# One adaLN / HGRN2 / stick-breaking / SwiGLU layer in float32: GpSimd's elementwise work on VectorE, conditioning rows in one operation each, 1 MB loads in a ring of 8 KB tiles

## The chip, the cores and the metric

The kernel runs on one core of one Trainium2 chip. The metric is the device time of one execution in microseconds (us). A core has TensorE (PE, matmuls; PEld is its weight load), VectorE (DVE), ScalarE (ACT), GpSimd (POOL) and SyncE (SP), which issues the DMAs of this kernel. The "granted clock" is the share of TensorE's full clock that the profile shows for a stretch.

## The reference

One layer, 512 tokens, width 2048, hidden width 5632, all float32. Cut to what matters:

```python
cond = silu(c)
mod = cond @ w_ada + b_ada                     # 6 rows of 2048: sh1, sc1, g1, sh2, sc2, g2
h = rms_norm(x, norm1_g) * (1 + sc1) + sh1
proj = h @ w_in                                # columns: hgrn2 q, f, i, g; attention q, k, v
o_hg = hgrn2_mixer(...)                        # gated linear recurrence, 8 heads of 128
o_sb = stick_breaking_mixer(...)               # causal stick-breaking attention, 8 heads of 128
x = x + g1 * (concat(o_hg, o_sb) @ w_out)
h = rms_norm(x, norm2_g) * (1 + sc2) + sh2
gate, up = split(h @ w_ffn_in)
x = x + g2 * ((silu(gate) * up) @ w_ffn_out)
```

The product cond @ w_ada is a matrix times one vector; it reads 100 MB for 12288 sums.

## The kernel before, in words

**Matmuls in pieces.** TensorE multiplies a float32 matrix in a reduced form, so each operand is split into a high part (a cast, on ACT) and the remainder (a subtraction, mostly on DVE). A product is three matmuls: high x high, high x low, low x high (`three`, L207). `weights` (L197) loads a piece of 512 KB at most (`raw`, a ring of four tiles of 4 KB per partition, shared by nearly all loads of the kernel), casts it (L203) and subtracts (L204). A new load waits until the tile four loads before it has been read for the last time; SP issues in order, so a load that waits holds up those behind it.

**Conditioning rows.** `gemv` (L179) makes one row of 128 sums: two halves of 512 KB on SP (L176), for each a multiply with `cond` that also sums (L183), into half_a and half_b. `ada` adds the halves and b_ada (L189) and for the two scale rows makes the gain (L192). There are 96 such rows and 14 more of the same form (`fix`).

**Stages in order of time.** A, `st`, L265 to L297: 16 steps over the input width for the `i` columns of all HGRN2 heads, with one SC1 row, one piece of x and 512 KB of weights per step and 24 matmuls 512 wide. x isn't normalised yet; the sums of squares are gathered beside it, ss1, by GpSimd (L288). B: `sb_project(0)` and `sb_project(1)`, q, k and v of attention heads 0 and 1, eight chunks of 24 matmuls 384 wide each (tiles wsb_0 to wsb_7, accumulated in sbp). Beside them run, as side tasks, the 16 SH1 rows and `first_norm`, in which GpSimd multiplies x by the row norm rb (L471). When these are done, hhi and hlo, TensorE's operand, are rewritten with the normalised and shifted input (L486 to L488). C: `sb_project` of heads 2 to 7, and all attention (`sb_attend`: transposes tA and tB, products sbo; L373 scales q and k, L345 the output). In C the parts that A and B computed from the raw input are repaired: `spread` writes a row to memory and reads it back on all partitions (drow), `fix` makes 14 rows with it, and `settle` adds the result to heads 0 and 1 and to the `i` columns. Then HG (HGRN2, eight heads), `wo` (output projection; `split_o`, L773, splits the mixer's output, odd pieces on GpSimd), a first part of the FFN, the FFN loop over f = 2 to 43 (seven products of 24 matmuls 256 wide per f, from sums and differences of the weight quarters), and `fo`, the last product.

**Order.** The order in which TensorE takes projection, attention and repair work is made when the program is written out: a planner's clock counts matmul time, and a side task (a generator) goes on when the clock has reached the time that it asked for. Y holds these delays; "settle" is the one between the last fix of a group and its settle. A head whose rows reuse a buffer waits for the head that holds it (`reuse`, L307: head 3 waits for head 0).

Of the kernel before, what the change touches and what calls it, by code (L numbers as in the profile page):

```python
# [128 lines left out]
def trunk(ctx, tc, a):  # L129
# [41 lines left out]

    ahead = {}

    def gemv_load(src, i, name):
        w = raw_tile([P, 1024], f"{name}_{i}")
        nc.sync.dma_start(w, src[:, i * 1024:i * 1024 + 1024])  # L176
        return w

    def gemv(src, row, col_a, col_b, name):  # L179
        for i, col in enumerate((col_a, col_b)):  # L180
            w = ahead.pop((name, i)) if (name, i) in ahead else gemv_load(src, i, name)
            sl = slice(i * 1024, i * 1024 + 1024)
            V.scalar_tensor_tensor(w, w, 1.0, row[:, sl], op0=ALU.mult, op1=ALU.mult, accum_out=col)  # L183

    def ada(comp, k):
        j = comp * KT + k
        c = slice(j, j + 1)
        gemv(a["w_ada"][j], cond, half_a[:, c], half_b[:, c], f"ada{j}")
        V.scalar_tensor_tensor(mod[:, c], half_a[:, c], half_b[:, c], small_col(C_BADA, j), op0=ALU.add, op1=ALU.add)  # L189
        if comp in (SC1, SC2):  # L190
            g, base = (gain1, C_N1) if comp == SC1 else (gain2, C_N2)
            V.scalar_tensor_tensor(g[:, k:k + 1], mod[:, c], 1.0, small_col(base, k), op0=ALU.add, op1=ALU.mult)  # L192

    def mcol(comp, k):
        return mod[:, comp * KT + k:comp * KT + k + 1]

    def weights(src, shape, name):  # L197
        r = raw_tile(shape, name + "r")
        nc.sync.dma_start(r, src)
        hi = wp.tile(shape, F32R, tag="hi", name=name + "h")  # L200
        lo = wp.tile(shape, F32R, tag="lo", name=name + "l")
        with tc.high_priority(offset=AHEAD):
            S.copy(hi, r)  # L203
            V.tensor_sub(lo, r, hi.bitcast(F32))  # L204
# [60 lines left out]
    for k in range(KT):  # L265
        xk = xo[:, k]
        if k == 0:
            ada(SC1, k)
            whi = wp.tile([P, 1024], F32R, tag="hi", name="wi0h")
            wlo = wp.tile([P, 1024], F32R, tag="lo", name="wi0l")  # L270
            for sl in (slice(0, T), slice(T, 2 * T)):
                S.copy(whi[:, sl], w0[:, sl])
                V.tensor_sub(wlo[:, sl], w0[:, sl], whi[:, sl].bitcast(F32))
        else:
            nc.sync.dma_start(xk, a["x"][:, k])
            ada(SC1, k)
            if k == 2:
                nc.sync.dma_start(cst, a["cst"])
            whi, wlo = weights(a["w_hi"][k], [P, 1024], f"wi{k}")
        gk = gain1[:, k:k + 1]  # L280
        S.activation(hhi[:, k], xk, AF.Identity, scale=gk)
        V.scalar_tensor_tensor(hlo[:, k], xk, gk, hhi[:, k].bitcast(F32), op0=ALU.mult, op1=ALU.subtract)
        if k == 0:
            S.activation(ss1, xk, AF.Square)
        else:
            sq = sb.tile([P, T], F32, tag="qT" if k % 2 else "kT", name=f"sq{k}", bufs=1)
            S.activation(sq, xk, AF.Square)
            G.tensor_add(ss1, ss1, sq)  # L288
# [49 lines left out]
    def row_norm_scale(o_ps, name, pool, tp=None):  # L338
# [4 lines left out]
        y = rstd_small(pool, ss, 4, name)  # L343
        for t in range(4):
            V.tensor_scalar(orow[:, t], o_ps[:, t * P:t * P + P], y[:, t:t + 1], None, op0=ALU.mult)  # L345
        yield Y["norm"]
# [13 lines left out]
    def sb_prepare(h):  # L360
# [9 lines left out]
        y = rstd_small(sb, ss, 8, f"sb{h}")  # L370
        for t in range(4):
            for j in range(2):
                V.tensor_scalar(rows[:, t, j * P:j * P + P], rows[:, t, j * P:j * P + P],  # L373
                                y[:, 2 * t + j:2 * t + j + 1], None, op0=ALU.mult)

# [91 lines left out]
    def first_norm():  # L467
        ps = att("ssum")
        rstd_wide(sb, ss1, ps, "n1", ("qT", "L"), 1, rb)
        for k in range(KT):  # L470
            G.tensor_mul(xo[:, k], xo[:, k], rb)  # L471
# [301 lines left out]
    def split_o(k):  # L773
        S.copy(ohi[:, k], xo[:, k])
        (G if k % 2 else V).tensor_sub(olo[:, k], xo[:, k], ohi[:, k].bitcast(F32))
# [103 lines left out]

    def operand(raw, name):  # L880
        hi = wp.tile([P, HALF, P], F32R, tag="hi", name=name + "h")
        lo = wp.tile([P, HALF, P], F32R, tag="lo", name=name + "l")
        with tc.high_priority(offset=AHEAD):
            S.copy(hi, raw)  # L884
            V.tensor_sub(lo, raw, hi.bitcast(F32))
        return hi, lo

    def load_block(pool, tag, bufs, f, g, kh):
        r = pool.tile([P, HALF, P], F32, tag=tag, name=f"ff{f}_{g}{kh}", bufs=bufs)
        nc.sync.dma_start(r, a["w_fi"][f, g][:, kh * HALF:kh * HALF + HALF])  # L890
        return r

    def product(out, w, p, first=False):
# [241 lines left out]
```

## Time and profile before

| What | us |
|---|---|
| median of three runs (2403.39 to 2404.9) | 2404.03 |
| the profiled execution | 2405.08 |
| its span in the profile (granted clock 0.993) | 2403.3 |
| A begins | 11.2 |
| B begins | 109.2 |
| C begins | 200.7 |
| HG begins | 484 |
| wo begins | 818 |
| FFN loop begins | 1067.3 |
| fo begins | 1920 |

The table's boundaries are the first matmuls of each stage by the timeline, and the windows of the prediction are cut at them. Between the span and the execution's time lie 1.8 us. A row of the timeline reads: start, duration, engine, line, operation, out<-in, shapes, count, and in brackets how long the engine had been idle and what ended that. Successive rows of DVE can overlap by some tens of ns, so the cost of one in a busy row is taken from start to start.

### The profile page before, as it was taken

Reading aid. Unit: us, or ns where it says so; the run is one execution under the profiler, and the core shown is the slowest. Engines: PE = TensorE matmul, PEld = TensorE weight load, DVE = VectorE, ACT = ScalarE, POOL = GpSimd, SP = SyncE. Lnnn points to the kernel's source line nnn. Section 1 sums busy time; section 2 is a strip of 40 time slices with the busy share of each in tenths; the row PEclk is TensorE's granted clock in tenths of the full one; section 3 lists DMA queues with packets and bytes.
Section 4 is the critical chain, followed back from the end, with each engine's and each line's share of the span. In section 5 each row is a group of like instructions: output and inputs, shape, how many; then the busy total and the mean of one; then the engine's idle time right before and its main releaser. Section 6 shows DMA issues by size and latency. Waiting matters only on the chain.

```text
span 2403.3 us, 36514 instructions
## 1 busy us (share of the span) xinstructions
PE 2321.8 (97%) x14371; PEld 2106.9 (88%) x14371; DVE 1701.3 (71%) x2585; ACT 1033.9 (43%) x1833; POOL 82.6 (3%) x64
## 2 busy tenths in 40 slices
PE   7989898999999999989999999999999999999999
PEld 6778788978888778889999999999999988888887
DVE  8997888789888875598888877777777633333332
ACT  4343664466565522374444444444444421122221
POOL 2250000000000200000000000000000000000000
PEclk9999999999999999999999999999999999999999
DMA  8878546743332286535555533333333484363342
GB/s 316 278 248 262 191 156 224 238 165 115 106 106 97 79 266 219 188 121 178 185 184 185 182 135 131 129 130 130 131 132 132 170 327 155 101 198 95 106 127 88
DMA packets 122488, 403.10 MB, mean 168 GB/s; under 512 B 13614, under 2 KB 14284, under 8 KB 122188
## 3 DMA queue, kind: packets, MB, share of 16 engines
q1 hardware_dynamic: 122316, 400.77, 49.8%
q8 instruction: 112, 1.84, 0.3%
q14 instruction: 60, 0.49, 0.1%
HBM read 369.24 MB, written 31.47 MB: 167 GB/s over the span
## 4 chain that ended last, share of the span: by engine, by line
PE 75%; DVE 10%; DMA 9%; issue 3%; ACT 2%; POOL 0%; POOLq 0%; SPq 0%; ACTq 0%; DVEq 0%
PE ffA L92 20%; PE fo L92 20%; PE ffC L92 10%; PE wo L92 6%; PE ffB L92 5%; DMA ada<-in_w_ada 4%; PE hgg L92 3%; DVE ada L183 3%; PE hgf L92 3%; PE hgq L92 3%; PE ff L92 1%; DMA fix<-in_w_fix 1%; DVE I L413 1%; PE l L92 1%; PE hgo L92 1%
## 5 line engine op out<-in xcount | busy, mean ns | idle before, releaser
L183 DVE SCALAR_TENSOR_TENSOR ada<-ada,cond 128x1024 f32<-128x1024 f32 x192 | 260.5, 1366 | 94.9 <-DMA ada<-in_w_ada 94.6
L92 PE MATMUL fo<-act,wfo_0h 128*128 128x512 f32 x1024 | 315.4, 389 | 0.0
L92 PEld LDWEIGHTS fo<-act,wfo_0h 128*128 128x128 f32 x1024 | 192.2, 188 | 39.9
L92 PE MATMUL fo<-act,wfo_0l 128*128 128x512 f32 x512 | 199.2, 389 | 0.0
L204 DVE TENSOR_TENSOR wfo_8l<-wfo_8r,wfo_8h 128x512 fp32r<-128x512 f32 x48 | 33.2, 692 | 177.6 <-ACT wfo_8h L203 177.6
L1071 DVE SCALAR_TENSOR_TENSOR x<-fo,mod,x 128x512 f32<-128x512 f32 x64 | 48.1, 751 | 131.2 <-PE fo L92 127.2
L203 ACT CAST wfo_0h<-wfo_0r 128x1024 fp32r<-128x1024 f32 x64 | 67.7, 1058 | 164.9 <-PE fo L92 142.1
L92 PE MATMUL ffA<-opA,ff_1h 128*128 128x256 f32 x672 | 124.6, 286 | 6.1 <-DVE up L1001 6.1
L92 PE MATMUL ffA<-opB,ff_6h 128*128 128x256 f32 x672 | 124.0, 285 | 2.1 <-ACT ff_6h L884 2.1
L92 PE MATMUL ffC<-opB,ff_7h 128*128 128x256 f32 x672 | 123.1, 283 | 0.4 <-ACT ff_7h L884 0.4
L92 PE MATMUL ffB<-opA,ff_2h 128*128 128x256 f32 x672 | 122.8, 283 | 0.0
L92 PE MATMUL ffA<-opC,ff_5h 128*128 128x256 f32 x672 | 122.8, 283 | 0.0
L92 PE MATMUL ffC<-opC,ff_4h 128*128 128x256 f32 x672 | 122.8, 283 | 0.0
L92 PE MATMUL ffA<-opD,ff_3h 128*128 128x256 f32 x672 | 122.8, 283 | 0.0
L203 ACT CAST wfo_8h<-wfo_8r 128x512 fp32r<-128x512 f32 x48 | 30.0, 624 | 210.3 <-PE fo L92 210.3
L92 PE MATMUL fo<-act,wfo_8h 128*128 128x512 f32 x384 | 118.2, 389 | 0.0
L92 PEld LDWEIGHTS fo<-act,wfo_0l 128*128 128x128 f32 x512 | 96.1, 188 | 19.9
L92 PEld LDWEIGHTS ffA<-opA,ff_1h 128*128 128x128 f32 x672 | 106.4, 195 | 6.3 <-issue 6.3
L92 PEld LDWEIGHTS ffA<-opB,ff_6h 128*128 128x128 f32 x672 | 105.9, 194 | 2.3 <-ACT ff_6h L884 2.3
L92 PEld LDWEIGHTS ffC<-opB,ff_7h 128*128 128x128 f32 x672 | 104.9, 192 | 0.7 <-ACT ff_7h L884 0.7
L92 PEld LDWEIGHTS ffB<-opA,ff_2h 128*128 128x128 f32 x672 | 104.8, 192 | 0.0
L92 PEld LDWEIGHTS ffA<-opC,ff_5h 128*128 128x128 f32 x672 | 104.8, 192 | 0.0
(691 smaller groups left out, 6727.1 us busy)
## 6 DMA issues: line engine op xcount, KB each, us to landing
ada<-in_w_ada SPq DMA_DIRECT2D x192, 512.0 KB, 4.5
ff<-in_w_fi SPq DMA_DIRECT2D x168, 512.0 KB, 3.6
wfo_0r<-in_w_fo SPq DMA_DIRECT2D x64, 512.0 KB, 3.6
actd<-pair SPq DMA_DIRECT2D x44, 512.0 KB, 2.6
act<-actd SPq DMA_DIRECT2D x44, 512.0 KB, 6.2
fix<-in_w_fix SPq DMA_DIRECT2D x28, 512.0 KB, 4.9
wfo_8r<-in_w_fo SPq DMA_DIRECT2D x48, 256.0 KB, 2.7
wo_8r<-in_w_out SPq DMA_DIRECT2D x16, 512.0 KB, 4.4
```

Source lines behind the costliest of these rows:

```text
L92: self.engine.matmul(out, lhsT, rhs, **kw)
L183: V.scalar_tensor_tensor(w, w, 1.0, row[:, sl], op0=ALU.mult, op1=ALU.mult, accum_out=col)
L203: S.copy(hi, r)
L204: V.tensor_sub(lo, r, hi.bitcast(F32))
L413: V.tensor_tensor_scan(Ig[:, ::-1], seg[:, base:base + width][:, ::-1], Lg[:, ::-1], 0.0, op0=ALU.mult, op1=ALU.add)
L1071: V.scalar_tensor_tensor(x2[m], out, mcol(G2, m), x2[m], op0=ALU.mult, op1=ALU.add)
```

## The change

1. GpSimd's sums (ss1), products (xo by rb) and remainders (olo) are made by DVE. GpSimd keeps the memsets.
2. A conditioning row is one load of 1 MB (8 KB per partition) and one multiply-and-sum over 2048 elements straight into its column of mod. b_ada is added for all 16 columns of a component at once when its last row is in (for SC1 still one by one), and the second gain likewise. Only the very first row is still in two halves. The addition of ba and bb falls away with the halves.
3. Weights come in loads of 1 MB or 768 KB (pairs of chunks of w_sb, whole tiles of w_hg, w_out and w_ffn_in, a chunk's whole row of w_ffn_out); each is split in halves as before. The raw ring has four tiles of 8 KB per partition; the FFN's second ring (raw2, five tiles of 4 KB) becomes "sum", two of 4 KB.
4. The scalings per head: one multiply by a broadcast column in place of eight (L373, now L391) or four (L345, now L364).
5. Y["settle"] goes from 8 to 20. The program is also built with dynamic_dma_scratch_size=256.

Lines move: load L176 to L174, gemv L183 to L178, weight load L199 to L205, cast and subtraction L203/L204 (in the FFN L884/L885) to L212/L213, xo by rb L471 to L488, hlo L488 to L505, sums of the FFN quarters L1011 to L1014 to L1022 to L1025.

```diff
-     "settle": 8.0, "shrow": 6.0, "fix": 2.6, "hgtask": 30.0, "task": 5.0}
+     "settle": 20.0, "shrow": 6.0, "fix": 2.6, "hgtask": 30.0, "task": 5.0}
...
-    def gemv(src, row, col_a, col_b, name):
-        for i, col in enumerate((col_a, col_b)):
-            w = ahead.pop((name, i)) if (name, i) in ahead else gemv_load(src, i, name)
-            sl = slice(i * 1024, i * 1024 + 1024)
-            V.scalar_tensor_tensor(w, w, 1.0, row[:, sl], op0=ALU.mult, op1=ALU.mult, accum_out=col)
+    def row_load(src, name):
+        w = raw_tile([P, D], name)
+        nc.sync.dma_start(w, src)
+        return w
+
+    def gemv(w, row, col):
+        V.scalar_tensor_tensor(w, w, 1.0, row, op0=ALU.mult, op1=ALU.mult, accum_out=col)
...
+        gemv(row_load(a["w_ada"][j], f"ada{j}"), cond, mod[:, c])
+        left[comp] -= 1
+        if comp == SC1:
+            V.tensor_add(mod[:, c], mod[:, c], small_col(C_BADA, j))
+            finish_gain(comp, k, k + 1)
+        elif not left[comp]:
+            all_k = slice(comp * KT, comp * KT + KT)
+            V.tensor_add(mod[:, all_k], mod[:, all_k], small[:, C_BADA + comp * KT:C_BADA + comp * KT + KT])
...
-            G.tensor_add(ss1, ss1, sq)
+            V.tensor_add(ss1, ss1, sq)
...
-            whi, wlo = weights(a["w_sb"][h, c], [P, 2, 384], f"wsb{h}_{c}")
+            if c % 2 == 0:
+                raw = load(a["w_sb"][h, c // 2], [P, 2, 2, 384], f"wsb{h}_{c}")
+            whi, wlo = split(raw[:, c % 2], [P, 2, 384], f"wsb{h}_{c}")
...
-        for t in range(4):
-            V.tensor_scalar(orow[:, t], o_ps[:, t * P:t * P + P], y[:, t:t + 1], None, op0=ALU.mult)
+        V.tensor_mul(orow, o_ps.rearrange("p (t d) -> p t d", t=4), view(y, 0, [[1, 4], [0, P]]))
...
+        qk = rows[:, :, 0:2 * P].rearrange("p t (j d) -> p t j d", j=2)
+        V.tensor_mul(qk, qk, view(y, 0, [[2, 4], [1, 2], [0, P]]))
...
-            G.tensor_mul(xo[:, k], xo[:, k], rb)
+            V.tensor_mul(xo[:, k], xo[:, k], rb)
...
-        gemv(a["w_fix"][j], shrow, ba[:, j:j + 1], bb[:, j:j + 1], f"fix{j}")
+        gemv(row_load(a["w_fix"][j], f"fix{j}"), shrow, ba[:, j:j + 1])
...
-        (G if k % 2 else V).tensor_sub(olo[:, k], xo[:, k], ohi[:, k].bitcast(F32))
+        V.tensor_sub(olo[:, k], xo[:, k], ohi[:, k].bitcast(F32))
...
-        A11, A12 = (load_block(wp, "raw", 4, f, 0, kh) for kh in range(2))
-        A21, A22 = (load_block(tp, "raw2", 5, f, 1, kh) for kh in range(2))
-        S1 = tp.tile([P, HALF, P], F32, tag="raw2", name=f"ffS{f}", bufs=5)
+        A11, A12 = halves_of(load(a["w_fi"][f, 0], [P, KT, P], f"wg{f}"))
+        A21, A22 = halves_of(load(a["w_fi"][f, 1], [P, KT, P], f"wu{f}"))
+        S1 = tp.tile([P, HALF, P], F32, tag="sum", name=f"ffS{f}")
```

DVE in stage B at head 1's chunks, before (ada_0 and ada_1 are the two halves of a row, wsb_4l the remainder of the fourth chunk of weights, hlo the rewritten operand):

```order
L204 TENSOR_TENSOR wsb_4l<-wsb_4r,wsb_4h 128x768
L189 SCALAR_TENSOR_TENSOR mod<-half_a,half_b,small 128x1
L183 SCALAR_TENSOR_TENSOR ada_0_1353,half_a<-ada_0_1353,cond 128x1024
L488 TENSOR_TENSOR hlo<-xo,hhi 128x512
L183 SCALAR_TENSOR_TENSOR ada_1_1356,half_b<-ada_1_1356,cond 128x1024
L488 TENSOR_TENSOR hlo<-xo,hhi 128x512
L204 TENSOR_TENSOR wsb_5l<-wsb_5r,wsb_5h 128x768
```

A row's two halves and two rewrites stand between the remainders of two chunks. After, at head 0's chunks, where GpSimd multiplied before (rb is the row norm, rcolT its transpose):

```order
L178 SCALAR_TENSOR_TENSOR ada_945,mod<-ada_945,cond 128x2048
L488 TENSOR_TENSOR xo<-xo,rb_783 128x512 x2
L213 TENSOR_TENSOR wsb_4l<-wsb_4r,wsb_4h 128x768
L213 TENSOR_TENSOR wsb_5l<-wsb_4r,wsb_5h 128x768
L488 TENSOR_TENSOR xo<-xo,rb_783 128x512 x12
L213 TENSOR_TENSOR wsb_6l<-wsb_6r,wsb_6h 128x768
L213 TENSOR_TENSOR wsb_7l<-wsb_6r,wsb_7h 128x768
L488 TENSOR_TENSOR xo<-xo,rb_783 128x512 x2
L494 COPY rcol<-rcolT 128x1 x4
L178 SCALAR_TENSOR_TENSOR ada_978,mod<-ada_978,cond 128x2048
```

The two subtractions of a pair of chunks stand together, the products of xo are among them, and the 16 rewrites of hlo have moved behind the last SH1 row, into stage C.

TensorE at the attention of head 0, before, around its second group of transposes tB (tA is the first group, sbo the products with the values, spread belongs to a settle, sbp is projection work):

```order
L97 MATMUL tB_2080<-cst,I_1844 128x128
L92 MATMUL sbp_1_1869<-wsb_4h,hlo 128x384
L92 MATMUL sbp_2_1870<-wsb_4h,hhi 128x384
L92 MATMUL sbp_2_1870<-wsb_4l,hhi 128x384
L92 MATMUL sbp_2_1870<-wsb_4h,hlo 128x384
L92 MATMUL sbp_3_1871<-wsb_4h,hhi 128x384
L92 MATMUL sbp_3_1871<-wsb_4l,hhi 128x384
L92 MATMUL sbp_3_1871<-wsb_4h,hlo 128x384
L92 MATMUL sbp_0_1868<-wsb_5h,hhi 128x384
L97 MATMUL tB_2080<-cst,L_1843 128x128
```

Projection matmuls of head 3 stand between its steps here. After, from the first transposes tA on:

```order
L92 MATMUL sbp_3_1660<-wsb_7h,hhi 128x384
L92 MATMUL sbp_3_1660<-wsb_7l,hhi 128x384
L97 MATMUL tA_1908<-cst,I_1789 128x128 x2
L97 MATMUL tA_1908<-cst,L_1788 128x128
L97 MATMUL tA_1908<-cst,I_1789 128x128
L92 MATMUL sbp_3_1660<-wsb_7h,hlo 128x384
L92 MATMUL sbo_1932<-scr,L_1788 128x128 x4
L97 MATMUL spread_2016<-cst,ba 3x128
L97 MATMUL tB_1965<-cst,I_1789 128x128
L97 MATMUL tB_1965<-cst,L_1788 128x128
```

Head 0's attention stood inside a projection; now it stands at the end of head 3's, with one projection matmul between its steps.

VectorE in the FFN loop after, from a gemv to the first use of the next f's weights (wu8r, whose tile of the ring the gemv's row had held; ffS is the sum of its halves):

```order
L178 SCALAR_TENSOR_TENSOR ada_10265,mod<-ada_10265,cond 128x2048
L1025 TENSOR_TENSOR wg7r<-wg7r 128x1024
L213 TENSOR_TENSOR ff_6l<-wg7r,ff_6h 128x1024
L1001 TENSOR_TENSOR sg_10022<-sg_10022,up_10023 128x512
L213 TENSOR_TENSOR ff_7l<-wu7r,ff_7h 128x1024
L1004 TENSOR_TENSOR pair_10030<-sg_10022,pair_10030 128x512
L1040 TENSOR_TENSOR sg_10253<-ffB_10043,a_10081 128x256
L1022 TENSOR_TENSOR ffS_10272<-wu8r 128x1024
```

Six operations stand between the two. Before, a row came in two halves at two places of the loop, and the weights of the second block had a ring of their own.

More of the change, by code (lines that the diff above doesn't have):

```diff
@@ L158, in trunk @@
     G.memset(epsb, EPS)
-    half_a = const.tile([P, 96], F32, name="half_a")
-    half_b = const.tile([P, 96], F32, name="half_b")
+    lead = const.tile([P, 2], F32, name="lead")
+    left = [KT] * 6
     mod = const.tile([P, 96], F32, name="mod")
@@ L170, in raw_tile, with finish_gain @@
         return wp.tile(shape, F32, tag="raw", name=name, bufs=4)
[L172 to L176, printed above, removed]
-        return w
-    def gemv(src, row, col_a, col_b, name):
-        for i, col in enumerate((col_a, col_b)):
-            w = ahead.pop((name, i)) if (name, i) in ahead else gemv_load(src, i, name)
-            sl = slice(i * 1024, i * 1024 + 1024)
-            V.scalar_tensor_tensor(w, w, 1.0, row[:, sl], op0=ALU.mult, op1=ALU.mult, accum_out=col)
+    def row_load(src, name):
+        w = raw_tile([P, D], name)
+        nc.sync.dma_start(w, src)
+        return w
+    def gemv(w, row, col):
+        V.scalar_tensor_tensor(w, w, 1.0, row, op0=ALU.mult, op1=ALU.mult, accum_out=col)
+    def finish_gain(comp, k0, k1):
+        g, base = (gain1, C_N1) if comp == SC1 else (gain2, C_N2)
+        V.scalar_tensor_tensor(g[:, k0:k1], mod[:, comp * KT + k0:comp * KT + k1], 1.0, small[:, base + k0:base + k1],
+                               op0=ALU.add, op1=ALU.mult)
     def ada(comp, k):
@@ L187, in ada, with load, split @@
         c = slice(j, j + 1)
[L188 to L192, printed above, removed]
+        gemv(row_load(a["w_ada"][j], f"ada{j}"), cond, mod[:, c])
[6 more added lines that the diff above has]
+            V.tensor_add(mod[:, all_k], mod[:, all_k], small[:, C_BADA + comp * KT:C_BADA + comp * KT + KT])
+            if comp == SC2:
+                finish_gain(comp, 0, KT)
     def mcol(comp, k):
+        assert comp == SC1 or not left[comp]
         return mod[:, comp * KT + k:comp * KT + k + 1]
-    def weights(src, shape, name):
+    def load(src, shape, name):
         r = raw_tile(shape, name + "r")
         nc.sync.dma_start(r, src)
+        return r
+    def split(r, shape, name):
         hi = wp.tile(shape, F32R, tag="hi", name=name + "h")
@@ L205, in weights @@
         return hi, lo
+    def weights(src, shape, name):
+        return split(load(src, shape, name), shape, name)
     def three(out, whi, wlo, xhi, xlo, start, stop):
@@ L252, in trunk @@
     banks += [wide[:, 0:T], wide[:, T:2 * T]]
+    r0 = raw_tile([P, D], "ada_first")
     for i in range(2):
@@ L255, in trunk @@
         nc.sync.dma_start(cond[:, sl], a["c"][:, sl])
-        ahead[f"ada{SC1 * KT}", i] = gemv_load(a["w_ada"][SC1 * KT], i, f"ada{SC1 * KT}")
+        nc.sync.dma_start(r0[:, sl], a["w_ada"][SC1 * KT][:, sl])
         S.activation(cond[:, sl], cond[:, sl], AF.Silu)
@@ L267, in trunk @@
         if k == 0:
-            ada(SC1, k)
+            for i in range(2):
+                sl = slice(i * 1024, i * 1024 + 1024)
+                gemv(r0[:, sl], cond[:, sl], lead[:, i:i + 1])
+            j = SC1 * KT
+            V.scalar_tensor_tensor(mod[:, j:j + 1], lead[:, 0:1], lead[:, 1:2], small_col(C_BADA, j), op0=ALU.add, op1=ALU.add)
+            finish_gain(SC1, 0, 1)
             whi = wp.tile([P, 1024], F32R, tag="hi", name="wi0h")
@@ L370, in sb_prepare @@
         y = rstd_small(sb, ss, 8, f"sb{h}")
[L371 to L374, printed above, removed]
+        qk = rows[:, :, 0:2 * P].rearrange("p t (j d) -> p t j d", j=2)
+        V.tensor_mul(qk, qk, view(y, 0, [[2, 4], [1, 2], [0, P]]))
     def sb_attend(h):
@@ L495, in trunk @@
     ba = const.tile([P, 14], F32, name="ba")
-    bb = const.tile([P, 14], F32, name="bb")
     def spread(dst, cols, n0, n1):
@@ L513, in settle @@
         yield Y["settle"]
-        V.tensor_add(ba[:, n0:n1], ba[:, n0:n1], bb[:, n0:n1])
         spread(brow, ba, n0, n1)
@@ L575, in mtile @@
         n = 0
+        raw = load(src, [P, nk, P], name)
         for c0 in range(0, nk, HALF):
             w = min(HALF, nk - c0)
-            whi, wlo = weights(src[:, c0:c0 + w], [P, w, P], f"{name}_{c0}")
+            whi, wlo = split(raw[:, c0:c0 + w], [P, w, P], f"{name}_{c0}")
             for kk in range(w):
@@ L774, in split_o @@
         S.copy(ohi[:, k], xo[:, k])
-        (G if k % 2 else V).tensor_sub(olo[:, k], xo[:, k], ohi[:, k].bitcast(F32))
+        V.tensor_sub(olo[:, k], xo[:, k], ohi[:, k].bitcast(F32))
     for k in list(range(8, 16)) + list(range(last)):
         split_o(k)
-    wo, wo_n, wo_w = {}, {}, {}
+    wo, wo_n, wo_w, wo_raw = {}, {}, {}, {}
     def wo_part(m, c0, ks):
@@ L785, in wo_part @@
         if (m, c0) not in wo_w:
-            wo_w[m, c0] = weights(a["w_out"][m][:, c0:c0 + 8], [P, 8, P], f"wo{m}_{c0}")
+            if m not in wo_raw:
+                wo_raw[m] = load(a["w_out"][m], [P, KT, P], f"wo{m}")
+            wo_w[m, c0] = split(wo_raw[m][:, c0:c0 + 8], [P, 8, P], f"wo{m}_{c0}")
         whi, wlo = wo_w[m, c0]
@@ L878, in make_second @@
         parts[1, 1, j] = H[3][:, j, 0], H[3][:, j, 1]
[L880 to L891, printed above, removed]
     def product(out, w, p, first=False):
@@ L980, in trunk, with halves_of, operand @@
     actd = [dram.tile([P, 2, T], F32, name=f"actd{f}") for f in range(FM)]
+    def halves_of(r):
+        return r[:, 0:HALF], r[:, HALF:KT]
+    def operand(raw, name):
+        return split(raw, [P, HALF, P], name)
     def tap(src, name):
@@ L1060, in trunk @@
             n = 0
+            raw = load(a["w_fo"][m][:, f0:f0 + size], [P, size, P], f"wfo{c}_{m}")
             for c0 in range(0, size, HALF):
                 w = min(HALF, size - c0)
-                whi, wlo = weights(a["w_fo"][m][:, f0 + c0:f0 + c0 + w], [P, w, P], f"wfo{c}_{m}_{c0}")
+                whi, wlo = split(raw[:, c0:c0 + w], [P, w, P], f"wfo{c}_{m}_{c0}")
                 for kk in range(w):
@@ L1090 @@
     w_in = get["w_in"][0]
-    w_sb = w_in[:, 4096:].reshape(8, 2, P, 3, NH, P).transpose(4, 0, 2, 1, 3, 5).reshape(NH, 8, P, 2, 384)
+    w_sb = w_in[:, 4096:].reshape(4, 2, 2, P, 3, NH, P).transpose(5, 0, 3, 1, 2, 4, 6).reshape(NH, 4, P, 2, 2, 384)
     hgm = mtiles(w_in[:, :4096], KT).reshape(4, NH, P, KT, P)
@@ L1123 @@
     }
-    nc = bacc.Bacc("TRN2", target_bir_lowering=False, num_devices=1)
+    nc = bacc.Bacc("TRN2", target_bir_lowering=False, num_devices=1, dynamic_dma_scratch_size=256)
     args = {n: nc.dram_tensor(f"in_{n}", v.shape, mybir.dt.from_np(v.dtype), kind="ExternalInput").ap()
```

## The prediction

> **What bounds the kernel now.** I read the page's head first, then windows cut at the stages, then the timelines of VectorE and GpSimd inside the slow stages, and last the list of waits.
>
> ```profile
> span 2403.3 us, 36514 instructions
> PE 2321.8 (97%) x14371; PEld 2106.9 (88%) x14371; DVE 1701.3 (71%) x2585; ACT 1033.9 (43%) x1833; POOL 82.6 (3%) x64
> ```
>
> TensorE is 97% busy, so the whole kernel looks bound by it and GpSimd looks irrelevant. Both are averages. The windows by stage (columns: stretch, length, busy us of PE, PEld, DVE, ACT, POOL, granted clock, DMA share, GB/s) say where it isn't so:
>
> ```profile
> 11.20:109.20 98.00, 93.58 (x385) 72.85 (x386) 90.40 (x132) 37.00 (x51) 24.51 (x15) 1.00 0.88 303
> 109.20:200.70 91.50, 76.74 (x401) 69.69 (x400) 83.78 (x124) 39.50 (x57) 34.57 (x16) 0.98 0.79 254
> 1200.00:1240.00 40.00, 40.00 (x336) 40.00 (x335) 34.72 (x43) 19.40 (x28) 0.00 (x0) 1.00 0.53 181
> ```
>
> In the FFN loop (third row) TensorE has no gap, and nothing that the change does to the other engines can pay there. In stage A (the values of eight heads, 16 steps) and stage B (the projections of heads 0 and 1) VectorE is busy 92% of the time, TensorE 95% and 84%. What would TensorE need alone? Its rows start one behind the other, first two of stage A, then two of an undisturbed 384-wide stretch:
>
> ```profile
> 69.38 0.39 PE L92 MATMUL st<-wi9h,hhi 128*128 128x512 f32 x1
> ...
> 71.87 0.39 PE L92 MATMUL st<-wi9h,hlo 128*128 128x512 f32 x1
> ```
> ```profile
> 201.85 0.33 PE L92 MATMUL sbp<-wsb_0h,hhi 128*128 128x384 f32 x1
> ...
> 204.28 0.33 PE L92 MATMUL sbp<-wsb_1h,hlo 128*128 128x384 f32 x1
> ```
>
> Eleven matmuls in 2.49 us are 0.226 us each, and 14 in 2.43 us are 0.174. Stage A has 16 x 24 of the first: 87 us, where it takes 98. Stage B has 2 x 8 x 24 of the second: 67, where it takes 91.5. So 11 and 25 us are above TensorE's floor. What takes them shows in VectorE's and GpSimd's timelines, first for a step of A:
>
> ```profile
> 73.54 2.31 DVE L183 SCALAR_TENSOR_TENSOR ada<-ada,cond 128x1024 f32<-128x1024 f32 x1
> ...
> 75.78 1.21 DVE L183 SCALAR_TENSOR_TENSOR ada<-ada,cond 128x1024 f32<-128x1024 f32 x1
> ```
> ```profile
> 72.98 1.79 POOL L288 TENSOR_TENSOR ss<-ss,sq 128x512 f32<-128x512 f32 x1 [4.31 <-ACT sq L287]
> ```
>
> The same product takes 2.31 us where it meets GpSimd's sum and 1.21 where it doesn't: 1.1 us lost per step. In stage B GpSimd multiplies without a break (16 products, 34.6 us, below), and VectorE reads:
>
> ```profile
> 134.42 1.09 DVE L189 SCALAR_TENSOR_TENSOR mod<-half_a,half_b,small 128x1 f32<-128x1 f32 x1
> 135.44 0.94 DVE L204 TENSOR_TENSOR wsb_4l<-wsb_4r,wsb_4h 128x768 fp32r<-128x768 f32 x1
> 136.31 2.30 DVE L183 SCALAR_TENSOR_TENSOR ada<-ada,cond 128x1024 f32<-128x1024 f32 x1
> ...
> 138.54 2.31 DVE L183 SCALAR_TENSOR_TENSOR ada<-ada,cond 128x1024 f32<-128x1024 f32 x1
> ...
> 141.90 0.94 DVE L204 TENSOR_TENSOR wsb_5l<-wsb_5r,wsb_5h 128x768 fp32r<-128x768 f32 x1
> ...
> 154.83 1.22 DVE L183 SCALAR_TENSOR_TENSOR ada<-ada,cond 128x1024 f32<-128x1024 f32 x1
> ...
> 157.59 0.21 DVE L189 SCALAR_TENSOR_TENSOR mod<-half_a,half_b,small 128x1 f32<-128x1 f32 x1
> ...
> 166.25 0.69 DVE L488 TENSOR_TENSOR hlo<-xo,hhi 128x512 fp32r<-128x512 f32 x1
> 166.85 1.22 DVE L183 SCALAR_TENSOR_TENSOR ada<-ada,cond 128x1024 f32<-128x1024 f32 x1
> ```
>
> A chunk takes 6.46 us (135.44 to 141.90), with VectorE back to back, against 24 x 0.174 = 4.2 of TensorE. Once GpSimd is done the three long operations cost 1.22, 1.22 and 0.21. So stage B has VectorE, slowed by GpSimd, as its bound until 154. After that it waits for loads:
>
> ```profile
> 160.51 1.22 DVE L183 SCALAR_TENSOR_TENSOR ada<-ada,cond 128x1024 f32<-128x1024 f32 x1 [0.97 <-DMA ada<-in_w_ada]
> ```
> ```profile
> 155.00:200.00 45.00, 40.93 (x218) 37.23 (x219) 39.40 (x69) 25.51 (x39) 0.00 (x0) 1.00 0.87 280
> ```
>
> **The change part by part.**
>
> *GpSimd's work on VectorE.* The groups that go:
>
> ```profile
> L471 POOL TENSOR_TENSOR xo<-xo,rb 128x512 f32<-128x512 f32 x16 | 34.6, 2198 | 18.9 <-DVE rb L215 18.9
> L288 POOL TENSOR_TENSOR ss<-ss,sq 128x512 f32<-128x512 f32 x15 | 24.5, 1634 | 72.5 <-ACT sq L287 72.5
> L775 POOL TENSOR_TENSOR olo<-xo,ohi 128x512 fp32r<-128x512 f32 x8 | 13.5, 1705 | 48.8 <-ACT ohi L774 48.7
> ```
>
> A 128x512 operation costs VectorE 0.60 from start to start (166.25 to 166.85). Stage A: 15 x (1.09 lost - 0.60 added), and mod, gain and one accumulator read in fewer pieces, bring 90.4 us of VectorE to about 82. Stage B: 83.8 - 16 x 1.09 + 16 x 0.60 - some 13 rewrites of hlo (0.60 each, moved behind the last SH1 row, which is in stage C) = 68. The Trainium skill, page "SBUF — State Buffer", Terms, has it that VectorE and GpSimd share a pair of ports and that the loser is blocked for the whole instruction. Read as GpSimd's full 2.2 us, 35 us would come back in B; the trace shows 1.09 per meeting, and wsb_4l at 0.94 is not stretched at all, so the sum goes by 1.09. In VectorE's new order twelve of the products stand in a row between wsb_5l and wsb_6l, 7.2 us in which no weight is split; the two chunks ahead keep TensorE busy for 48 x 0.174 = 8.4, so I count nothing, and 1 to 2 us if it reaches them early.
>
> *Loads.* VectorE out of the way, A needs 98.0 x 303 = 29.7 MB and B 91.5 x 254 = 23.2 MB. At full share these rates are 303 / 0.88 = 344 and 254 / 0.79 = 321 GB/s: 86 and 72 us. The other end is what the same queue moves when it never pauses, with 512 KB loads:
>
> ```profile
> 1945.00:1950.00 5.00, 5.00 (x24) 4.14 (x23) 1.89 (x3) 1.06 (x1) 0.00 (x0) 1.00 1.03 406
> ```
>
> At 406 they need 73 and 57. No row shows 8 KB rows, so I take the lower rates, A's and B's own. The Trainium skill, page "DMA: Bandwidth & Descriptors", Bandwidth, tells to batch up to 1 MiB, with 341 GB/s there. By that figure the loads would be A 87 and B 68, and the size would be the gain; the row above has 406 with half the size, so I count nothing for size itself.
>
> So A: TensorE 87, VectorE 82, loads 86; three limits this close, and a ring of four, won't fit perfectly: 91.5, **-6.5** (-3 to -11). B: 67, 68, 72: I take 75, **-16.5** (-10 to -23).
>
> *Between B and C* all 16 SH1 rows get b_ada in one addition, so that no xo of head 2 can be rewritten before the last row is in: one gemv (two halves, 2.3), addition, two ACT passes and a subtraction before head 2's first matmul. With half of it covered, **+2** (0 to +4).
>
> *Stage C (heads 2 to 7).* Three things. First, fixes in whole rows: SP no longer queues weights behind fix halves that wait for shrow. Before, this cost
>
> ```profile
> 210.00:215.00 5.00, 2.53 (x13) 1.96 (x13) 4.21 (x7) 0.83 (x1) 0.00 (x0) 0.97 0.65 193
> 215.00:220.00 5.00, 5.00 (x21) 5.00 (x22) 2.91 (x6) 0.84 (x1) 0.00 (x0) 0.69 0.88 323
> ```
>
> 2.5 us of idle and a granted clock of 0.69 for 5 us (1.5 us): **-4** (0 to -5), since the ring now holds two chunks per tile. Second, "settle" at 20 puts head 0's attention behind almost all of head 3's projection, with one projection matmul left between tA and the last sbo. Before, it ran with some 36 between:
>
> ```profile
> 264.13 0.44 PE L97 MATMUL tA<-cst,I 128*128 128x128 f32 x2 [2.02 <-ACT I L419]
> ...
> 271.74 1.60 PE L92 MATMUL sbo<-scr,L 128*128 128x128 f32 x12
> ```
>
> 9.2 us from the first to the end of the last; 36 x 0.174 = 6.3 of it was projection work that now stands elsewhere, and the chain through ACT remains: **+6** (+3 to +9). Third, scalings:
>
> ```profile
> 247.68 1.66 DVE L373 TENSOR_SCALAR scr<-scr,ysb 128x128 f32<-128x128 f32 x8
> ```
> ```profile
> 851.46 1.12 DVE L345 TENSOR_SCALAR orowhg<-hgo,yhg 128x128 f32<-128x128 f32 x4
> ```
> ```profile
> PE qkt L97 <- DVE rows L373: 8.9, 6, 2.1
> PE ffA L92 <- DVE up L1001: 6.1, 1, 6.1
> ...
> PE wo L92 <- DVE olo L775: 2.9, 2, 2.2
> ...
> PE otpsb L97 <- DVE orowsb L345: 2.6, 3, 1.6
> ...
> PE ffA L92 <- ACT ff_6h L884: 2.1, 1, 2.1
> ...
> PE wo L92 <- POOL olo L775: 2.0, 2, 1.4
> ```
>
> One operation over 1024 elements at 1.22 for the eight, one over 512 at 0.75 (estimate: 0.69 of L488 and a little, as its input is in PSUM) for the four: 0.44 on six waits for rows and 0.37 on three for orow: 2.6 + 1.1, of which I take **-3** (0 to -4). Stage C together **-1** (-6 to +8).
>
> *wo.* GpSimd's remainders go; VectorE makes all 16 at 0.60, and isn't stretched meanwhile. Of the waits for olo (2.9 and 2.0) **-3** goes (-1 to -5).
>
> *FFN.* At the start, gemv and sum stand ahead of the copies of "up" (2.3 us longer for the 6.1) and the second wait, 2.1, goes: **0** (-3 to +3). In the loop the 1 MB load of wu waits for the slot that the gemv frees. Behind the gemv stand six operations (three of 1.14 from start to start, 0.60, 0.60, 0.33) ahead of the first use: 4.9 us, and VectorE's own idle time, 40.00 - 34.72 over two f, is 2.6 per f: 7.5 us of cover. Half such a load landed in
>
> ```profile
> ada<-in_w_ada SPq DMA_DIRECT2D x192, 512.0 KB, 4.5
> ```
>
> 4.5 us; another 0.5 MB at 406 GB/s is 1.3, so 5.8 (estimate; at worst twice 4.5): **0**. HG and the last product: 0, TensorE has no gaps that end at a load there.
>
> Sum: -6.5 - 16.5 + 2 - 1 - 3 = **-25**. The profiled execution took 2405.1 (span 2403.3 and 1.8 around it), 1.0 above the median of the runs. 2404 - 25 = **2379**.
>
> **The rivals.**
>
> *Loads as fast as TensorE.* At 406 GB/s A and B fall to TensorE's floor plus the start: A -10, B -22, the rest as above: -34, 2370. For it: the row at 1945. Against it: A and B didn't reach it at full share (344, 321). By the 341 GB/s of the Trainium skill's page "DMA: Bandwidth & Descriptors", Bandwidth, A would lose 11 and B 23, the same time nearly; no run shows it for such loads yet.
>
> *Loads don't speed up.* The queue stays at what it moved with its pauses, 303 in A and in B 280 to 303: A 0, B 23.2 MB / 290 = 80, -11, and the clump in C costs its full 9 with no saving beside it, +2 between: A and B -11, C +9, boundary +2, wo -3: -3, 2401. For it: after 155 us, GpSimd gone, VectorE waits on ada loads. Against: the ring was 2 MB deep and is 4.
>
> *Slower: the FFN ring.* If a 1 MB load lands later than 7.5 us after the gemv frees its slot, each of 16 f loses the excess L - 7.5. The rest gains 25, so it decides from L = 7.5 + 25 / 16 = 9.1; at 9.5 it is 32 - 25 = +7, 2411. For it: twice 4.5 is 9.0. Against: the loop moves 181 GB/s at share 0.53, so queues are short.
>
> *The stretch is not GpSimd's.* If those 2.3 us were the product's own price here, VectorE would carry 15 x 0.60 more in A (+1 there) and B would gain only by the moved hlo: about -3 in all, 2401. Against: 154.83, 1.22, the moment that GpSimd stops.
>
> **How the numbers follow.** Forecast 0.66, faster loads 0.17, unchanged loads 0.09, FFN ring 0.06, stretch not GpSimd's 0.02. A measurement here can tell 0.2% (4.8 us). Faster takes the first two (0.83), same the third and fifth (0.11), slower the fourth (0.06). The forecast's own bounds are about 2366 to 2395; taking in the faster loads and the poor end of C, the range is 2364 to 2396, with some 0.17 outside.
>
> **What would show it.** Right: every product of 2048 near 2.3 us in A, B and later (one operation for what was 2.31 + 1.21); stage A near 91 us and B near 75; the share of the DMA in B above 0.9; TensorE's wait at 213 gone, a new one of 5 to 8 us at head 0's tA and tB; FFN loop still 20.1 us per f. Wrong: products that remain stretched; A above 96 or B above 82; waits of TensorE for ff_5 or ffS in f 2 to 17; more than 10 us lost in C.

## The result and the profile after

The changed kernel takes 2342.72 us (median of four, 2342.37 to 2343.62), the kernel before 2404.47 (median of four): a ratio of 0.9744, 95% interval 0.9727 to 0.9761, 62 us less. The forecast was 2379 within 2364 to 2396: the direction was right and the size far too small. The profiled execution took 2343.62, 1.8 of it outside its span. The head of its page:

```profile
span 2341.8 us, 35224 instructions
PE 2303.9 (98%) x14371; PEld 2106.8 (90%) x14371; DVE 1646.8 (70%) x2208; ACT 1027.8 (44%) x1833; POOL 10.7 (0%) x25
```

TensorE's busy time has changed by 18 us and the span by 61.5: what is gone is mostly idle time of TensorE. The windows by stage of the kernel after (columns as in the prediction) show A, B, C and the FFN loop, and below them stands C of the kernel before, which the prediction didn't show:

```profile
11.50:100.60 89.10, 89.10 (x384) 73.36 (x385) 80.28 (x116) 38.80 (x52) 0.00 (x0) 1.00 0.95 360
100.60:175.00 74.40, 71.38 (x392) 70.09 (x391) 64.45 (x78) 18.83 (x27) 0.00 (x0) 0.95 0.82 300
175.00:438.90 263.90, 256.37 (x1505) 243.54 (x1504) 211.08 (x296) 159.42 (x405) 0.00 (x0) 0.98 0.57 204
...
1009.80:1859.20 849.40, 849.40 (x7057) 849.40 (x7058) 670.46 (x711) 403.03 (x591) 0.00 (x0) 1.00 0.42 153
```
```profile
199.20:484.00 284.80, 258.06 (x1504) 240.49 (x1502) 225.59 (x458) 142.87 (x373) 0.00 (x0) 0.99 0.64 210
```

In C TensorE is busy for nearly the same time, 256 and 258 us; before, 27 us of the stage were idle, after, 7.5. Cut at the first matmul of each stage (B ends here at head 2's first matmul, 199.2 before; the prediction had cut 1.5 us later), in us:

| Stage | before | after | difference | forecast |
|---|---|---|---|---|
| A | 98.0 | 89.1 | -8.9 | -6.5 |
| B | 90.0 | 74.4 | -15.6 | -16.5 |
| C, with the boundary | 284.8 | 263.9 | -20.9 | +1 |
| HG | 334.0 | 330.5 | -3.5 | 0 |
| wo | 195.3 | 186.2 | -9.1 | -3 |
| FFN, first part and loop | 907.3 | 903.6 | -3.7 | 0 |
| fo | 482.7 | 482.7 | 0 | 0 |

A and B came out near their forecasts. The missing 37 us lie in C with HG (25), wo (6), the FFN's beginning (4) and A (2). The largest, C, shows in TensorE's waits there (columns: us in all, times, longest), before and then after:

```profile
PE qkt L97 <- DVE rows L373: 7.7, 5, 2.1
PE tA L97 <- ACT I L419: 5.6, 5, 2.0
PE sbp L92 <- DVE rows L331: 3.5, 3, 2.3
PE sbp L92 <- ACT wsb_3h L203: 1.9, 1, 1.9
```
```profile
PE tB L97 <- ACT I L440: 3.2, 1, 3.2
PE sbo L92 <- ACT L L454: 2.0, 3, 0.9
PE tA L97 <- ACT I L436: 1.4, 3, 0.7
...
PE qkt L97 <- DVE scr L391: 0.2, 1, 0.2
```

Before, TensorE waited in nearly every head for VectorE's results or for ACT's steps behind them; after, mostly at one place, the clump of head 0 (its attention steps one behind the other with hardly any projection between): 5.1 of the 7.5 us of idle time. What VectorE itself waited for in C, before and then after:

```profile
DVE ada L183 <- DMA ada<-in_w_ada: 23.4, 19, 2.9
DVE fix L183 <- DMA fix<-in_w_fix: 14.1, 12, 2.6
DVE fix L183 <- DMA xo<-drow: 5.5, 1, 5.5
```
```profile
DVE ada L178 <- DMA ada<-in_w_ada: 9.5, 7, 3.9
DVE wsb_0l L213 <- ACT wsb_0h L212: 7.2, 4, 5.2
```

In its timeline VectorE takes its operations in the order of the program, so a gemv that waits for its load holds up the scalings and scans of the attention behind it, and TensorE waits for these. One case from before:

```profile
399.42 1.23 DVE L183 SCALAR_TENSOR_TENSOR ada<-ada,cond 128x1024 f32<-128x1024 f32 x1 [1.11 <-DMA ada<-in_w_ada]
...
402.91 1.26 DVE L373 TENSOR_SCALAR rows<-rows,ysb 128x128 f32<-128x128 f32 x6
```
```profile
403.34 0.30 PE L97 MATMUL qkt<-cst,rows 128*128 128x128 f32 x1 [2.01 <-DVE rows L373]
```

Between the wait of 1.11 us and the scalings of rows stand the gemv itself, a second one, a remainder and the last two steps of the norm by which the rows are scaled. TensorE, which transposes the scaled rows, is idle for 2.01 us meanwhile. Before, the waits of the three lines above came to 43 us in C: 37.5 for loads of rows and 5.5 for the read-back of a spread row. After, those for rows came to 9.5.

The profile also follows the work that ended last back from step to step, each to what released it (inferred from semaphores). By line, as shares of C (the view cuts the lines off at their ends), before and then after:

```profile
by line: DMA ada<-in_w_ada 21.6%; DMA fix<-in_w_fix 10.8%; issue 10.3%; DVE ada L183 6.3%; DVE I L413 5.8%; DMA xo<-drow 4.3%; DVE I L414 3.7%; DVE fix L183 3.2%; DVE L L407 2.8%; DMA wsb_7r<-in_w_sb 2.0%; DMA wsb_5r<-in_w_sb 2.0%; ACT junk
```
```profile
by line: PE sbp L92 52.2%; PE sbo L92 6.0%; issue 4.8%; DVE fix L178 3.6%; DMA wsb_4r<-in_w_sb 3.0%; DVE I L430 2.7%; PE zA L92 2.7%; DVE L L424 2.4%; PE tB L97 2.3%; PE qkt L97 2.2%; PE zB L92 2.0%; DVE I L431 1.7%; DVE L L429 1.2%; DVE ws
```

Before, loads of rows made up about a third of this chain through C; after, it holds none of them, and TensorE's projection is half of it.

### The profile page after: what moved, and what is told of

It is laid out like the page before. It is cut to its first block, busy times and chain, and to the rows that moved or that the text cites. A ratio compares the mean times of both kernels' runs of the same rounds, so it can differ in the third digit from the quotient of the medians.

```text
span 2341.8 us, 35224 instructions
## 1 busy us (share of the span) xinstructions
PE 2303.9 (98%) x14371; PEld 2106.8 (90%) x14371; DVE 1646.8 (70%) x2208; ACT 1027.8 (44%) x1833; POOL 10.7 (0%) x25
## 4 chain that ended last, share of the span: by engine, by line
PE 90%; DVE 6%; ACT 2%; issue 1%; DMA 1%; SPq 0%; ACTq 0%; DVEq 0%
PE ffA L92 21%; PE fo L92 20%; PE ffC L92 10%; PE sbp L92 7%; PE wo L92 7%; PE ffB L92 5%; PE st L92 4%; PE hgf L92 4%; PE hgq L92 3%; PE hgg L92 3%; PE l L92 1%; PE sbo L92 1%; DVE ada L178 1%; PE hgo L92 1%; PE r L92 0%
## 5 line engine op out<-in xcount | busy, mean ns | idle before, releaser
L178 DVE SCALAR_TENSOR_TENSOR ada<-ada,cond 128x2048 f32<-128x2048 f32 x95 | 216.5, 2284 | 37.1 <-DMA ada<-in_w_ada 37.1
L92 PE MATMUL fo<-act,wfo_0l 128*128 128x512 f32 x512 | 199.2, 389 | 0.0
L92 PEld LDWEIGHTS ffC<-opC,ff_4h 128*128 128x128 f32 x672 | 104.8, 192 | 0.0
L92 PEld LDWEIGHTS ffA<-opD,ff_3h 128*128 128x128 f32 x672 | 104.8, 192 | 0.0
L92 PE MATMUL ffA<-opA,ff_1l 128*128 128x256 f32 x336 | 96.1, 286 | 0.0
```

The costliest lines, as they stand in the source:

```text
L92: self.engine.matmul(out, lhsT, rhs, **kw)
L178: V.scalar_tensor_tensor(w, w, 1.0, row, op0=ALU.mult, op1=ALU.mult, accum_out=col)
```

## The experiments

Theory D: the loads (depth of the ring, size) gave most, through VectorE's in-order waits for them. Rivals: G, GpSimd's work and the ports; S, the order that settle 20 gives; C, the scalings. Each run gives one time beside one of the kernel before on the same chip, which was 2405.3 to 2408.2, so the difference to that one is given, to be held against -61.8 of the change. The four runs of before spread over 2.0 us and those of after over 1.3, so a difference of 2 or 3 us between two such times is at the edge of what they can tell. The stage lengths are from the runs' own traces.

**x1, GpSimd's work back.** In the changed kernel three lines return:

```diff
-            V.tensor_add(ss1, ss1, sq)
+            G.tensor_add(ss1, ss1, sq)
-            V.tensor_mul(xo[:, k], xo[:, k], rb)
+            G.tensor_mul(xo[:, k], xo[:, k], rb)
-        V.tensor_sub(olo[:, k], xo[:, k], ohi[:, k].bitcast(F32))
+        (G if k % 2 else V).tensor_sub(olo[:, k], xo[:, k], ohi[:, k].bitcast(F32))
```

> The changed kernel with GpSimd's sums, products and odd remainders back on GpSimd; the rest of the change stays. Theory D (depth and size of the loads give most of C): A loses its 1.1 us per step again unless TensorE covers it, 3 to 7 us; B goes back to near 85 us, 10 us longer; C unchanged within 3 us; wo 3 to 9 longer; in all about 2362. Theory G (GpSimd gives nearly everything): above 2385, and C, in which GpSimd does nothing, unchanged too.

2348.69, -58.1. A 89.7, B 74.7, C and HG 594.0 (after: 594.4), wo 191.8. So A and B don't need it: only wo does, 5.6. Both theories had expected more. VectorE's timeline in B of this run, and the window of B:

```profile
118.59 2.05 DVE L213 TENSOR_TENSOR wsb_5l<-wsb_4r,wsb_5h 128x768 fp32r<-128x768 f32 x1
120.57 3.39 DVE L178 SCALAR_TENSOR_TENSOR ada<-ada,cond 128x2048 f32<-128x2048 f32 x1
...
123.89 3.37 DVE L178 SCALAR_TENSOR_TENSOR ada<-ada,cond 128x2048 f32<-128x2048 f32 x1
```
```profile
101.40:176.10 74.70, 69.51 (x393) 67.17 (x391) 70.28 (x62) 18.69 (x27) 42.13 (x16) 1.00 0.84 303
```

GpSimd still costs VectorE as much: beside its 16 products in B, 16 VectorE operations are stretched (a row 3.39 against 2.29, a subtraction 2.05 against 0.95). Added up as time above the usual one of the same operation and shape, that is 16.2 us here and 15.6 in the kernel before. But VectorE has less else to do in B, since the rewrites of hlo (9.6 us there before) have moved to C: with GpSimd's cost included it is busy 70.28 of the 74.70 us, and TensorE is idle for 5.2, as against 3.0 without GpSimd (above).

**x2, settle at 8; z3, at 14; z4, at 28.** One number in Y each.

```diff
-     "settle": 20.0,
+     "settle": 8.0,
```

> The changed kernel with Y settle at 8. Theory S (the order that 20 gives is what made C 19 us shorter): 2355 to 2362, C back by 10 or more. Theory D: within 5 us of 2343, the waits for scaled rows stay short, and the wait at head 0's tB (3.2 us) goes while one for the settled rows may come.

2351.01, -55.8: between the two theories. C and HG 599.6, so 5.2 come from the order, not the 10 of theory S, and the whole is 8 longer, not the 5 at most of theory D.

> The changed kernel with settle at 14, between 8 (2351) and 20 (2343): if head 0's attention behind head 3's projection is what helps, 2345 to 2351; if 14 already keeps TensorE from waiting for the settled rows and leaves projection work between head 0's steps, below 2342.

2348.2, -59.9; C and HG 596.9.

> The changed kernel with settle at 28: if a later settle only moves attention further back, 2345 or more (head 3's rows wait for head 0's end longer); if the waits of head 0's steps at tB and sbo come from fixes on VectorE, a further gain, 2340 or less.

2352.63, -55.5; C and HG 603.8, with waits at tB of 4.5 us in all. In both runs the first guess held and the second fell. 20 came out best of the four, 14 only 1.9 behind it.

**x3, the scalings in small operations again.**

```diff
-        V.tensor_mul(orow, o_ps.rearrange("p (t d) -> p t d", t=4), view(y, 0, [[1, 4], [0, P]]))
+        for t in range(4):
+            V.tensor_scalar(orow[:, t], o_ps[:, t * P:t * P + P], y[:, t:t + 1], None, op0=ALU.mult)
```

(and the eight of q and k likewise)

> The changed kernel with four and eight small scalings per head again. Theory C (scalings shorten the chain to qkt and otp, and that is C's gain): 2353 or more, the waits for rows back to 9 us in all. Theory D: 2343 to 2348, the prices alone (0.44 and 0.37 us per head).

2347.1, -59.7; C and HG 597.3, 2.9 longer: the prices of the operations, as forecast (-3). Theory C falls.

**x4, everything but the loads.** The kernel before with GpSimd's three lines on VectorE, the new scalings and settle 20.

> The kernel before with GpSimd's work on VectorE, one scaling per head and settle at 20, but its 512 KB loads, its ring of four tiles of 4 KB and its gemv in halves. Theory D: A and B gain 10 to 16 in all, C stays within 6 us of the 283 of before, VectorE still waits over 20 us for loads of ada and fix there; 2380 to 2392. Theories S and C: C falls to near 265; below 2370.

2401.61, -5.2. A 93.3, B 92.5, C 276.7, HG 339.3 (C and HG 616.1, before 618.8), wo 195.3. It is slower than theory D had it, theories S and C fall, and B is 2.4 longer than before. SP's and TensorE's waits around B's first chunks (columns as above):

```profile
SPq L176 <- DVE ada L183: 13.9, 5, 5.9
SPq L176 <- DMA wsb_3r<-in_w_sb: 3.9, 1, 3.9
```
```profile
PE sbp L92 <- ACT wsb_4h L203: 8.8, 1, 8.8
```

The products of xo stand in a row on VectorE; the gemvs behind them keep their tiles, SP waits for a tile with the weights of chunk 4 behind, and TensorE stops for 8.8 us. In the changed kernel, with the same row of products and the deeper ring, TensorE's longest wait in B is 1.8 us.

**y1 and y2, a deep ring of small tiles.** y1 is the kernel before with eight tiles of 4 KB, y2 has GpSimd's lines, scalings and settle of after as well; loads of 512 KB and gemv in halves in both.

```diff
-        return wp.tile(shape, F32, tag="raw", name=name, bufs=4)
+        return wp.tile(shape, F32, tag="raw", name=name, bufs=8)
...
-    nc = bacc.Bacc("TRN2", target_bir_lowering=False, num_devices=1)
+    nc = bacc.Bacc("TRN2", target_bir_lowering=False, num_devices=1, dynamic_dma_scratch_size=256)
```

> The kernel before, alone with a raw ring of eight tiles of 4 KB in place of four (and dynamic_dma_scratch_size=256, which makes the room); loads stay at 512 KB, GpSimd keeps its work. Theory D1 (bytes in flight: the ring's depth in MB is what counts): A, B and C fall as in the changed kernel, 2365 or less. Theory D2 (size of a load: fewer and longer ones are what counts): 2395 or more, with B still over 85.

2377.91, -27.4: between the two theories. A 92.4, B 82.8, C 274.4, HG 330.0, wo 193.8. In B VectorE waits for no load any more, and is busy 82.27 of the 82.8 us:

```profile
104.20:187.00 82.80, 74.68 (x392) 71.46 (x391) 82.27 (x121) 37.59 (x56) 34.56 (x16) 0.94 0.77 254
```

Here it is the bound, as the prediction said, and GpSimd's share becomes visible in y2:

> As the last, with GpSimd's work on VectorE, one scaling per head and settle at 20 as well: all of the change but the size of a load and the one-operation gemv. Theory D1: 2340 to 2352. Theory D2: 2385 to 2400.

2361.04, -44.2: between the two theories again. A 88.9, B 74.8, wo 186.5: all as in the changed kernel. C and HG 606.3, 12 short of it. So depth alone is not all.

**y3 and z2, two and three tiles of 8 KB** in the changed kernel (bufs=2, bufs=3).

> The changed kernel with two tiles of 8 KB in its ring: the depth of before, 2 MB, with loads of 1 MB. Theory D1: back to 2395 or more, B over 88, and worse where a row and weights alternate, since one tile is read while only one is loaded. Theory D2: 2350 to 2370.

2568.38, +163: A 121.6, B 94.3, FFN loop 961.8. Theory D1 holds and D2 falls. The number of tiles may count beside the bytes: A, where the FFN's second ring plays no part, took 98.0 us with 2 MB in the four tiles of before and takes 121.6 with 2 MB in two, of which one with weights is only half filled there.

> The changed kernel with three tiles of 8 KB: 3 MB. If what is in flight sets the pace, this lies between four tiles (2343) and two (2568), nearer to four: 2352 to 2400, with B between 75 and 94 and the FFN loop above 850. If four tiles are already more than enough: 2343 to 2348.

2399.93, -8.2: A 94.5, B 80.2, C and HG 607.1, loop 872.3. TensorE's waits in its FFN:

```profile
PE ffA L92 <- DVE ff_6l L213: 9.7, 5, 2.0
PE ffA L92 <- ACT sg L1011: 6.3, 1, 6.3
PE ffA L92 <- ACT a L995: 2.8, 4, 1.3
```

The 6.3 stands there with four tiles too. The others don't; with three tiles the loop loses 23 us. This is the FFN's ring, of which the prediction's third rival spoke, though TensorE waits at ff_6 and a, not at ff_5 or ffS.

**y4, a row in two operations of 1024 from its one load, and an addition.**

```diff
-        V.scalar_tensor_tensor(w, w, 1.0, row, op0=ALU.mult, op1=ALU.mult, accum_out=col)
+            for i, out in enumerate((col, hb)):
+                sl = slice(i * 1024, i * 1024 + 1024)
+                V.scalar_tensor_tensor(w[:, sl], w[:, sl], 1.0, row[:, sl], op0=ALU.mult, op1=ALU.mult, accum_out=out)
+            V.tensor_add(col, col, hb)
```

> The changed kernel with each conditioning row multiplied in two operations of 1024 from the one load, and added: the operation count of before (one more addition), the loads of after. If the count of VectorE's operations matters: 2352 or more, mostly in A (16 x 0.4 = 6). If only the loads do: 2343 to 2350.

2346.31, -59.0, in the range for the loads alone: C and HG 597.7, 3.3 longer, A 89.7.

**z1, two DMAs into each tile.**

```diff
-        nc.sync.dma_start(w, src)
+        for i in range(2):
+            sl = slice(i * 1024, i * 1024 + 1024)
+            nc.sync.dma_start(w[:, sl], src[:, sl])
```

(weights likewise)

> The changed kernel with every load of 1 MB or 768 KB issued as two DMAs into the same tile: the transfers of before with the ring and the operations of after. If the size of a DMA counts: 2352 or more. If only tiles and operations do (what is in flight, and what SP waits for between): 2342 to 2347.

2349.42, -58.7, between the two forecasts: A 90.0, B 74.3, C and HG 598.6 (4.2 longer, in HG), the rest as after. By this run the size of a DMA is worth some 3 us of the 62, at the edge of what it can tell; in HG it is one wait of TensorE for scaled rows, 4.3 us.

**w1 and w2, C's rows without loads.** To see whether C is held by waits for loads, the 24 rows of G1 and SC2 in C are multiplied from cond, which is resident; tiles and operations stay. These rows' values, and what is made of them, are not the reference's.

```diff
+            if name in unloaded:
+                w = raw_tile([P, 1024], f"{name}_{i}")
+                V.scalar_tensor_tensor(w, cond[:, sl], 1.0, row[:, sl], op0=ALU.mult, op1=ALU.mult, accum_out=col)
+                continue
```

> The kernel before, with the 24 conditioning rows of G1 and SC2 that run in stage C multiplied from resident data: VectorE's work and the ring's tiles as before, their 24 MB of loads left out (so these rows' values are not the reference's). If VectorE's in-order waits for loads are what holds C in the kernel before: C from 285 to 270 or less, TensorE's waits for scaled rows from 8 us to under 4. If C is bound by the amount of VectorE's work or by the order: C stays above 280.

The kernel before with that: 2387.66, -20.5. C 269.7 (before 284.8), C and HG 598.8 (618.8), all other stages within 1.3. TensorE's waits for scaled rows fall from 7.7 to 4.8, less far than expected:

```profile
PE qkt L97 <- DVE rows L378: 4.8, 4, 1.5
PE sbp L92 <- ACT wsb_3h L208: 3.2, 1, 3.2
```

The run takes 24 MB off the queue as well as the waits off VectorE. That weights come earlier is not what pays: TensorE's waits for weights in C are all at one chunk 3, with 3.7 us here and 2.5 before.

> The same rows without loads in the kernel with eight tiles of 4 KB and the rest of the change (2361): if the 12 us in C and HG that this still lacks against the changed kernel are waits for loads too, C and HG fall from 606 to 597 or less; if they come from the count of operations and of tiles, they stay above 602.

y2 with that: 2344.69, -63.5: C and HG 589.0, 17 less than y2. So loads hold C in both; with order, scalings and VectorE's other work unchanged, leaving out these loads gives 20 and 17 us.

## Why the prediction was wrong

**What bounds A and B: half right, and the sum right in part by luck.** The prediction named VectorE, slowed by GpSimd, as B's bound until 154. The stretching is real (2.29 without GpSimd, 3.39 with it), but in B it was one of two limits of about the same height: the products' move alone gave nothing (x4 92.5, because of the row of products), a deep ring alone 7 (82.8), both 15 (74.8); and with the rest of the change in place GpSimd costs B nothing (x1 74.7). The forecast of B came out because both limits went, not because GpSimd's share was what it was taken for. In A the two cures add up: 5 (x4 93.3), 6 (y1 92.4), both 9 (y2 88.9, within 2 us of TensorE's floor of 87).

**"At full share these rates are 344 and 321."** This failed: the changed kernel moved 360 GB/s in A at a share of 0.95 and 300 in B at 0.82, which the same working makes 379 and 366. In A y2 came as high with loads of 512 KB:

```profile
11.60:100.50 88.90, 88.88 (x384) 73.23 (x385) 81.28 (x148) 36.94 (x51) 0.00 (x0) 1.00 0.94 358
```

So the rate of a queue with pauses, scaled up by its share, came out too low here. "I count nothing for size itself" held in A and B: y2, with 512 KB, has A 88.9 and B 74.8.

**"Stage C together -1": the step that failed.** A part was missing: VectorE's waits for the loads of fix and ada in C, 37.5 us before. The prediction had read waits for loads in B (the row at 160.51) and not asked what VectorE waits for in C, where it is busy 226 of 285 us and TensorE waits for it again and again. With the ring's depth alone changed, C and HG get 14.5 shorter (y1); with the loads of 24 rows alone left out, 20.0 (w1).

Of the three parts that the sum did have, the first and the third came in. The scalings were worth 2.9 (x3), for 3. The stall at 213, -4, is gone; a deeper ring is enough for that, since y1, with its halves of rows, has no idle time over 0.25 us in C before 230 either. The second part, +6 for settle at 20, has the wrong sign. The clump at head 0 is there:

```profile
252.81 0.48 PE L97 MATMUL tB<-cst,I 128*128 128x128 f32 x1 [3.17 <-ACT I L440]
```

From the first tA (247.04) to the end of the last sbo (258.47) it takes 11.4 us with one projection matmul in it. Before, 9.2 us held 26 such matmuls by the trace, not the 36 that the prediction counted; without them, that is 4.7 before and 11.3 after, 6.6 longer. But the same delay saves more elsewhere in C: with settle at 8 (x2) TensorE waits 4.0 us at 212.93 for the fixes that a spread needs, and 3.1 at 216.28 for weights, and in all C and HG are 5.2 longer than with 20. (The upper end of the sum for C is +9 by its own parts, not +8.)

Of the 12 us from y2 to the changed kernel, one operation per row accounts for 3.3 (y4) and DMAs of 1 MB for 4.2 (z1); the other 4 stay open, and so does whether these parts add up. w2 shows that the loads of 24 rows cost y2 17 us, more than that gap. That the gap itself is such waits is argued, not shown: in y2 loads of ada and fix are 30.8% of the chain through C, in the changed kernel it holds none.

**wo, "-3": sized by the waits for olo alone.** It gained 9.1. Moving GpSimd's work without the ring gives 0 (x4, 195.3: waits for weights, wo_0l, take the place), the ring alone 1.5 (y1), both 8.8 (y2).

**FFN, "0".** The loop is as forecast: 20.16 us per f, before and after, in all but the first f. The first f took 26.74 before and 22.83 after: the waits at ff_6 and ff_7 (2.1 and 0.4) went as forecast, and the other 1.4 stand beside a granted clock of 0.81 before (1067.3 to 1087) and 0.85 after (1009.8 to 1030). The 2.3 added to the 6.1 didn't come, since TensorE waits for ACT there, 6.3:

```profile
PE ffA L92 <- ACT sg L1011: 6.3, 1, 6.3
```

The third rival's price was built on a landing of 5.8; 1 MB of a row landed in 5.2, the median over the whole kernel:

```profile
ada<-in_w_ada SPq DMA_DIRECT2D x95, 1024.0 KB, 5.2
```

Nothing was lost with four tiles, 23 us with three (z2). The rival "loads as fast as TensorE" was right for A (-8.9, for -10), and none of the rivals had VectorE's waits in C in it.

## What to carry to other kernels

Ask of every engine that works in order what it waits for, also in stages where it looks merely busy: a DMA wait on VectorE was here, some operations later, a wait of TensorE under another name. The profile's chain of the work that ended last shows it at once. Where two limits stand at about the same height, a cure for one alone can show little: here the two alone gave -5 and -27 us, and both -44. A ring's depth can be worth more than the work of an engine: the fourth tile of 8 KB was worth 54 us, and it may be more than a matter of megabytes, since 2 MB in two tiles were slower in A than 2 MB in four.

## What the runs showed of the hardware

Beside nearly every GpSimd sum or product (15 in A and 16 in B) one VectorE operation was stretched, long or short, mostly by about 1.1 us: a product of 1024 from 1.22 to 2.31, one of 2048 from 2.29 to 3.39, a 768-wide subtraction from 0.95 to 2.05, an operation on one column from 0.21 to 1.09. VectorE's operations being fewer and longer did not lessen that: beside GpSimd's 16 products in B, 16 of them were stretched in the kernel before and 16 in x1, by 15.6 and 16.2 us in all. One queue moved 358 GB/s with rows in loads of 512 KB (y2) and 360 with rows in loads of 1 MB (after), over 89 us of A.
